# The running sum of a depthwise convolution on VectorE: from SBUF to a two-bank PSUM tile

## The chip, the cores and the metric
The kernel runs on one core of one Trainium2 chip. The metric is the device time of one execution in microseconds (us), the median of several runs; lower is better. The kernel computes in fp32, with every matmul operand split into a high and a low part, so that most products are three matmuls.

## The reference, cut to what matters
A backbone of two layers over 512 latent and 256 context tokens of 1024 channels. Each layer projects its normed input into four head groups (attention, Fourier mixing, a convolution module, pooling), concatenates them, projects back, and runs a SwiGLU feed-forward. The part that the change touches is the convolution module:

```python
def conv_module(a, dw_w, dw_b, ln_g, ln_b, w_pw):
    glu = a[..., :W_CONV] * jax.nn.sigmoid(a[..., W_CONV:])
    y = lax.conv_general_dilated(glu, dw_w[:, None, :], window_strides=(1,),
        padding=[(CONV_WIDTH // 2, CONV_WIDTH // 2)],
        dimension_numbers=('NWC', 'WIO', 'NWC'), feature_group_count=W_CONV) + dw_b
    y = jax.nn.silu(layer_norm(y, ln_g, ln_b))
    return y @ w_pw
```

CONV_WIDTH is 31 and W_CONV is 256: each of 256 channels is summed over 31 shifted copies of its row, each with its own weight (a tap).

## The kernel before
Channels lie on the 128 partitions, so the 256 conv channels are two blocks. `mix_phase` does the token mixers of one layer, `ffn` the feed-forward. Within `mix_phase` the attention (24 tiles of 128 queries and one head in layer 0, 16 in layer 1) is written out step by step, and other work is handed out between its steps: TensorE work by `fill`, conv taps on VectorE by `pull`, conv taps on ScalarE and GpSimd by `side`. A scheduler then sets the final order on each engine, and each engine works through its own list in that order.

**The taps.** `conv_taps` (L551) computes, per block, `cacc = cacc + tap_j * glu[j : j + cwid]`, one VectorE instruction per tap over 783 columns in layer 0 (512 in layer 1, where only the latent tokens are left). Both tensors it reads, the gated input `glu` and the running sum `ca`, and the one it writes lie in SBUF. VectorE does 31 taps of the first block; of the second block the first 10 (layer 0) or 8 (layer 1) are done by `side_taps` (L568), with the products on ScalarE (`prod`) and the sums on GpSimd (L578), and VectorE adds the remaining 21 or 23. `conv_out` then transposes the sums (`lnT`), normalizes them and feeds the output projection (`wo`).

**The scores.** `Tile.soft` (L874) puts the scores of one tile (up to 768 columns) into a PSUM tile `S` of the pool tag `pb`, which has two buffers of two banks each. VectorE takes the row maximum from it (`st`, L886), ScalarE the exponentials (`pr`, L888); then the buffer is free again. `flip` (L892) transposes the result (`PT`) and multiplies by the values (`pv`). The K transposes (`kT`) that precede the attention use the same two buffers.

**Beside it.** GpSimd makes the low parts of weights (L105), the sums of `side_taps` (L578) and the windows of the pooling (L694, L707); TensorE also makes modulation vectors of a later step (`mod`, `mods`), pooled columns (`pp`), Fourier columns (`u`) and the Fourier products (`g`, `fp`, `fq`). The matmuls of every kind are recorded on L161, transposes on L167.

Of the kernel before, what the change touches and what calls it, by code (L numbers as in the profile page):

```python
# [35 lines left out]

# columns of the packed small vectors, per layer
V_G1, V_G2, V_BM, V_DB, V_LG, V_LB, V_PS, V_TAP, V_QG, V_KG, NV = \
    0, 8, 16, 64, 66, 68, 70, 72, 134, 198, 262

# pacing of the work that runs beside the attention, per layer: pieces of the conv columns that go before it, taps of the
# conv on VectorE before it, first step with taps, taps per step on VectorE and on ScalarE with GpSimd, amount of
# other TensorE work per step, the share of it between scores and values, taps of the conv's second block that ScalarE
# and GpSimd take
Pace = namedtuple("Pace", "cols taps0 step0 taps side fill share side_n")
# [4 lines left out]
def kernel(ctx: ExitStack, tc: tile.TileContext, xT, ctxT, vec, cst, dft,  # L50
# [13 lines left out]

    # working tiles by tag: (columns, buffers)
    tags = {f"x{k}": (768, 1) for k in range(KD)}
# [39 lines left out]

    # ------------------------------------------------------------------ constants
    vt = cp.tile([P, DEPTH * NV + 16], F32, name="vt")
# [31 lines left out]

    # silu(c), silu(c_ctx) as stationary operands padded to 32 columns
    scp = cp.tile([P, KD, 32], F32, name="scp")
# [9 lines left out]
    def behind(i, j):  # L152
        """i goes to its queue no earlier than j to its own"""
        tc.add_manual_dep(i.ins, j.ins.name, mybir.DependencyInfo(
            mybir.DependencyClass.NoSync, mybir.DependencyReason.DATA), reason="order")
# [19 lines left out]

    # ------------------------------------------------------------------ weights in order of use
    queue, ready = [], {}
# [104 lines left out]

    # ------------------------------------------------------------------ adaLN modulation
    def scaled_gain(l, i, k0, k1):
# [4 lines left out]
    def mod_pairs(l, q0, q1, mix=True):  # L289
        """pairs q0..q1 of modulation chunks: four groups of two contraction chunks side by side, then their sum"""  # L290
        def fetch_w(q):
            raws = []
            for k in range(0, KD if q < q1 else 0, 4 if mix else 3):
                raw = W("wm", F32) if mix else U("wm", "pr")
                n = min(KD - k, 4 if mix else 3)
                nc.sync.dma_start(out=raw[:, 0:256 * n].rearrange("p (k c) -> p k c", k=n),
                                  in_=rows(w_mod[l, P * k:P * k + P * n, 256 * q:256 * q + 256]))
                raws += [raw[:, 256 * i:256 * i + 256] for i in range(n)]
            return raws

        def finish(q, me):
            ps = PF("mods")
            for c in range(2):
                tr(ps[:, 128 * c:128 * c + 128], me[:, 128 * c:128 * c + 128], ident)
            m2 = modT[l][:, 2 * q:2 * q + 2, :]
            dve.tensor_reduce(out=m2, in_=ps[:, 0:256].rearrange("p (c g w) -> p c w g", c=2, g=4)[:, :, 0:2, :], axis=AX.X, op=ALU.add)
            dve.tensor_tensor(out=m2, in0=m2, in1=vcol(l, V_BM + 2 * q, 2).unsqueeze(2).to_broadcast([P, 2, 2]), op=ALU.add)
            if q // 4 in (1, 4):
                scaled_gain(l, q // 12, 2 * q % 8, 2 * q % 8 + 2)
        raws = fetch_w(q0)  # L310
        yield 0
        prev = None
        for q in range(q0, q1):
            ps = PF("mod")
            for k in range(KD):
                g = k % 4
                mm(ps[32 * g:32 * g + 32, 0:256], scp[:, k, :], raws[k],
                   start=k < 4, stop=k >= 4, tile_position=(0, 32 * g))
            raws = fetch_w(q + 1)
            if prev is not None:  # L320
                finish(*prev)
            me = S("me")
            act.copy(out=me[:, 0:256], in_=ps[:, 0:256])
            prev = q, me
            yield 1.0
        finish(*prev)

    def quarter_load(l, q):
        """columns of the first norm's shift and scale for contraction chunks 2q, 2q+1 of the mixers"""
        out = []  # L330
        for k in range(KD):
            if q % 2 == 0:
                if k % 2 == 0:
                    raw = W("wm", F32)
                v = raw[:, 512 * (k % 2):512 * (k % 2) + 512]
            else:
                v = U("wm", ("g0", "g1", "c0", "c1", "u0", "u1", "b0", "b1")[k])[:, 0:512]
            src = w_mod[l, P * k:P * k + P, 0:2048].rearrange("p (j c) -> p j c", j=2)
            nc.sync.dma_start(out=v.rearrange("p (j c) -> p j c", j=2), in_=src[:, :, 256 * q:256 * q + 256])
            out.append(v)  # L340
        return out
# [21 lines left out]

    # ------------------------------------------------------------------ RMS norms
    class Norm:
        """reciprocal RMS per token on all partitions; squares of chunks below `direct` are added off the tensor engine"""

# [64 lines left out]
    class Acts:  # L432
        """split activations, channels on partitions: latent and context tiles per channel chunk"""

# [14 lines left out]

    # ------------------------------------------------------------------ token mixers  # L450
    def rope_tables(l):
# [11 lines left out]
    def head_norm(t, ng, w):  # L463
        """rows of t hold ng groups of HD: divide each by its rms, in place"""
        sq = U("hsq", "t")
# [10 lines left out]
    def rope(t, na, nh, a0, i):  # L476
        """t: [P, na, nh, HD] of token chunks a0.., tables rtab[2i], rtab[2i+1]; in place"""
        w = na * nh * HD
# [16 lines left out]
    def mix_phase(l, norm, A, filler):  # L495
# [6 lines left out]

        # query, key and value columns: tokens on partitions, contraction outermost
        pl = [PB("qkv") for _ in range(2)]
# [21 lines left out]

        # Q: tile j holds latent chunks 2j, 2j+1 and context chunk 4+j; V split
        ksb = U("ksb", "a0")
# [19 lines left out]
        def tap(b, j):  # L548
            return vcol(l, V_TAP + CONVW * b + j)

        def conv_taps():  # L551
            for b in range(2):
                while done[0] <= b:
                    yield None
                if b:
                    for _ in side:
                        pass
                for j in range((0, pace.side_n)[b], CONVW):
                    if j == 0:
                        yield dve.tensor_scalar(out=cacc[b][:, :cwid], in0=glu[b][:, 0:cwid], scalar1=tap(b, 0),  # L560
                                                scalar2=vcol(l, V_DB + b), op0=ALU.mult, op1=ALU.add)
                    else:
                        yield dve.scalar_tensor_tensor(out=cacc[b][:, :cwid], in0=glu[b][:, j:j + cwid], scalar=tap(b, j),  # L563
                                                       in1=cacc[b][:, :cwid], op0=ALU.mult, op1=ALU.add)

            tdone[0] = True

        def side_taps():  # L568
            """the first taps of the second block: products on ScalarE, sums on GpSimd"""
            while done[0] < 2:  # L570
# [15 lines left out]

        # token-major columns
        def token_major(nm, chunks, sink, PS=PA):
# [18 lines left out]
        for j in range(2):  # L607
# [3 lines left out]
            rope(qsb[j], 2, 4, 2 * j, 0)  # L611
        # K stacks [k_hi;k_hi] and [k_lo;k_lo] over the 128 partitions
        K1 = [U(f"K1{h}", f"x{h}", F32R) for h in range(NKV)]
# [16 lines left out]

        # conv columns: output channels on partitions
        glu = [U(f"glu{b}", f"g{b}") for b in range(2)]
# [44 lines left out]

        # pooled columns: channels on partitions, zero-padded token axis
        ubs = [U(f"ub{b}", f"b{b}") for b in range(2)]
# [170 lines left out]

        # attention over tiles of 128 queries and one head, in three stages run two tiles apart
        qTs = {}
# [14 lines left out]
        class Tile:  # L867
            """128 queries of chunk q and one head"""

# [22 lines left out]
            def flip(self, pt_):  # L892
                """P transposed, the keys of chunks 0..3 in pt_[0] and of 4, 5 in pt_[1], each for two heads"""
                e = self.h % 2
# [127 lines left out]

        # output projection, gated residual, squares for the next norm
        n2 = Norm("b")
# [53 lines left out]

    # ------------------------------------------------------------------ SwiGLU
    def ffn(l, norm, first, second, A, filler):  # L1080
# [5 lines left out]
        def glu(c, pa_, pg, sl):  # L1086
            """h[:, sl] = silu(a) * g, split"""
            hh, hlo = h[c]
# [168 lines left out]
def _pack(i):  # L1257
    """small vectors laid out with channels on the partitions"""
    cols = []
# [38 lines left out]
```

## Time and profile before

| what | value |
|---|---|
| median of 3 runs | 1514.17 us (1511.99 to 1514.2) |
| profiled execution, span from first to last instruction | 1513.7 us (no other time is listed for it) |
| TensorE matmuls (PE) | 1455.2 us busy, 96% |
| weight loads (PEld) | 1210.9 us, 80% |
| VectorE (DVE) | 812.5 us, 54% |
| ScalarE (ACT) | 541.6 us, 36% |
| GpSimd (POOL) | 215.4 us, 14% |

The shares are means over the whole program. Layer 0's mixers run from about 75 to 300 us, its feed-forward to about 905 us, layer 1's mixers to about 1125 us, the rest is its feed-forward. [...] A wait is listed with what ended it.

### The profile page before, as it was taken

To read this page: it belongs to the slowest core of one execution; us is meant where nothing else is said; L and a number is where in the kernel's file an instruction comes from. 1 tells how busy PE (TensorE), PEld (TensorE's weight loads), DVE (VectorE), ACT (ScalarE), POOL (GpSimd) and SP (SyncE) were. 2 spreads that over 40 slices of the span, in tenths; PEclk is the share of its full clock that TensorE was granted. 3 is DMA by queue.
4 is the path that set the end of the run, shared out by engine and by line. 5 is a ranking of instruction groups with operands and counts; after the bars stand their busy time and mean duration, and the time that the engine had idled before them with its cause. 6 is when DMAs were issued, how large, how long until landed. Compare 5 with 4: busy or idle time off the path is not lost.

```text
span 1513.7 us, 20632 instructions
## 1 busy us (share of the span) xinstructions
PE 1455.2 (96%) x8538; PEld 1210.9 (80%) x8538; DVE 812.5 (54%) x1204; ACT 541.6 (36%) x876; POOL 215.4 (14%) x161
## 2 busy tenths in 40 slices
PE   7998899999999999999999999789999999999998
PEld 4786677888888888888888877577789888888887
DVE  3599884346543444344344357699446544444444
ACT  5456566534222112111211234557554322222220
POOL 2435520420000000000000024261140000000000
PEclk9998999999999999999999999999999999999999
DMA  8524344321222123212321222335832423333331
GB/s 297 166 91 138 116 156 124 90 70 57 84 84 84 59 81 111 85 52 88 98 85 56 70 98 56 125 113 162 250 91 73 123 88 94 97 98 97 98 98 56
DMA packets 192926, 157.35 MB, mean 104 GB/s; under 512 B 6464, under 2 KB 179520, under 8 KB 192832
## 3 DMA queue, kind: packets, MB, share of 16 engines
q1 hardware_dynamic: 192544, 155.34, 33.5%
q8 instruction: 67, 1.10, 0.3%
q10 hardware_dynamic: 288, 0.69, 0.1%
q14 instruction: 27, 0.22, 0.0%
HBM read 151.81 MB, written 4.19 MB: 103 GB/s over the span
## 4 chain that ended last, share of the span: by engine, by line
PE 80%; DVE 13%; DMA 3%; ACT 2%; issue 1%; POOL 1%; SPq 0%; DVEq 0%; ACTq 0%
PE ag L161 33%; PE fo L161 20%; PE agc L161 7%; PE wo L161 6%; DVE ca L563 6%; PE mod L161 3%; PE qkv L161 2%; PE ssq L161 2%; PE pv L161 1%; DVE st L886 1%; PE u L161 1%; DMA wi<-in_w_in_dram 1%; PE PT L167 1%; PE S L161 1%; DVE xt L426 1%
## 5 line engine op out<-in xcount | busy, mean ns | idle before, releaser
L1149 DVE SCALAR_TENSOR_TENSOR x<-fo,mod,x 128x512 f32<-128x512 f32 (+1 forms) x264 | 172.2, 661 | 138.4 <-PE fo L161 138.1
L161 PE MATMUL fo<-hh,foh 128*128 128x512 f32 (+1 forms) x528 | 188.2, 357 | 1.9 <-DVE ht L1092 1.9
L161 PE MATMUL fo<-hh,fol 128*128 128x512 f32 (+1 forms) x528 | 187.9, 356 | 0.0
L161 PE MATMUL fo<-hl,foh 128*128 128x512 f32 (+1 forms) x528 | 187.8, 356 | 0.0
L182 ACT CAST foh<-fo 128x1024 fp32r<-128x1024 f32 x44 | 46.2, 1049 | 275.2 <-PE fo L161 218.6
L161 PE MATMUL ag<-xfh,fah 128*128 128x512 f32 (+1 forms) x368 | 140.4, 386 | 1.2 <-ACT xfh L428 1.2
L161 PE MATMUL ag<-xfl,fah 128*128 128x512 f32 (+1 forms) x368 | 140.7, 382 | 0.8 <-DVE xfl L429 0.8
L161 PE MATMUL ag<-xfh,fal 128*128 128x512 f32 (+1 forms) x368 | 140.5, 382 | 0.0
L161 PE MATMUL ag<-xfh,fgh 128*128 128x512 f32 (+1 forms) x368 | 140.0, 381 | 0.0
L161 PE MATMUL ag<-xfh,fgl 128*128 128x512 f32 (+1 forms) x368 | 140.0, 380 | 0.0
L161 PE MATMUL ag<-xfl,fgh 128*128 128x512 f32 (+1 forms) x368 | 139.8, 380 | 0.0
L563 DVE SCALAR_TENSOR_TENSOR ca<-glu,vt,ca 128x783 f32<-128x783 f32 (+1 forms) x104 | 129.8, 1253 | 1.3
L161 PEld LDWEIGHTS fo<-hh,foh 128*128 128x128 f32 x528 | 98.9, 188 | 19.0 <-DVE ht L1092 2.1
L161 PEld LDWEIGHTS fo<-hl,foh 128*128 128x128 f32 x528 | 99.3, 188 | 16.7
L161 PEld LDWEIGHTS fo<-hh,fol 128*128 128x128 f32 x528 | 99.4, 188 | 15.7
L105 DVE TENSOR_TENSOR fal<-fa,fah 128x1024 fp32r<-128x1024 f32 x42 | 51.7, 1232 | 100.9 <-ACT fah L182 100.9
L105 DVE TENSOR_TENSOR fgl<-fg,fgh 128x1024 fp32r<-128x1024 f32 x42 | 51.4, 1225 | 97.6 <-ACT fgh L182 92.7
L182 ACT CAST fah<-fa 128x1024 fp32r<-128x1024 f32 x44 | 46.2, 1049 | 100.4 <-DMA fa<-in_w_ffn_in_dram 86.3
L182 ACT CAST fgh<-fg 128x1024 fp32r<-128x1024 f32 x44 | 46.1, 1048 | 98.5 <-DMA fg<-in_w_ffn_in_dram 88.2
L161 PEld LDWEIGHTS ag<-xfh,fah 128*128 128x128 f32 x368 | 69.0, 188 | 15.0 <-ACT xfh L428 1.4
L161 PEld LDWEIGHTS ag<-xfl,fah 128*128 128x128 f32 x368 | 69.2, 188 | 14.4 <-DVE xfl L429 1.7
L161 PEld LDWEIGHTS ag<-xfh,fgl 128*128 128x128 f32 x368 | 69.2, 188 | 13.1
(333 smaller groups left out, 3159.8 us busy)
## 6 DMA issues: line engine op xcount, KB each, us to landing
wm<-in_w_mod_dram SPq DMA_DIRECT2D x64, 512.0 KB, 4.7
fa<-in_w_ffn_in_dram SPq DMA_DIRECT2D x44, 512.0 KB, 3.9
fg<-in_w_ffn_in_dram SPq DMA_DIRECT2D x44, 512.0 KB, 3.9
fo<-in_w_ffn_out_dram SPq DMA_DIRECT2D x44, 512.0 KB, 3.3
wm<-in_w_mod_dram SPq DMA_DIRECT2D x40, 256.0 KB, 5.7
wo<-in_w_out_dram SPq DMA_DIRECT2D x16, 512.0 KB, 5.0
wm<-in_w_mod_dram SPq DMA_DIRECT2D x16, 384.0 KB, 5.8
x<-in_xT_dram SPq DMA_DIRECT2D x16, 256.0 KB, 4.4
```

The lines of the kernel that those rows point to most:

```text
L105: eng.tensor_tensor(out=out, in0=full, in1=b32(hi), op=ALU.subtract)
L161: i = last_pe[0] = pe.matmul(*a, **kw)
L167: i = last_pe[0] = pe.transpose(*a)
L182: act.copy(out=hi[:, :n], in_=raw[:, :n])
L426: dve.scalar_tensor_tensor(out=t[:, 0:n], in0=x[k][:, sl], scalar=aT[l][:, i, k, s:s + 1], in1=R[:, 0:n], op0=ALU.mult, op1=ALU.mult)
L563: yield dve.scalar_tensor_tensor(out=cacc[b][:, :cwid], in0=glu[b][:, j:j + cwid], scalar=tap(b, j), in1=cacc[b][:, :cwid], op0=ALU.mult, ...
L886: dve.tensor_reduce(out=st[:, 0:1], in_=ps[:, 0:kw], axis=AX.X, op=ALU.max, negate=True)
L1149: dve.scalar_tensor_tensor(out=x[m][:, sl], in0=ps[:, :n], scalar=modT[l][:, 40 + m, st:st + 1], in1=x[m][:, sl], op0=ALU.mult, op1=ALU.add)
```

## The change
The running sum of the taps that VectorE does is no longer kept in `ca` but in a PSUM tile `run`, taken from the tag `pb`, that is, one of the two buffers of the score tiles, for each block from its first VectorE tap to its last. The first tap writes `run` (in the second block it reads the ScalarE and GpSimd sum from `ca`), those between read and write `run`, and the last reads `run` and writes `ca`. So a tap in between reads one tensor from SBUF (`glu`) and one from PSUM. Comments are dropped too, and lines below L556 move by 3 (the taps are L562 and L565 afterwards, the row maximum L889).

```diff
+                run = PB("run")[:, :cwid]
+                j0 = (0, pace.side_n)[b]
+                for j in range(j0, CONVW):
-                for j in range((0, pace.side_n)[b], CONVW):
                     if j == 0:
-                        yield dve.tensor_scalar(out=cacc[b][:, :cwid], in0=glu[b][:, 0:cwid], scalar1=tap(b, 0),
+                        yield dve.tensor_scalar(out=run, in0=glu[b][:, 0:cwid], scalar1=tap(b, 0),
                                                 scalar2=vcol(l, V_DB + b), op0=ALU.mult, op1=ALU.add)
                     else:
-                        yield dve.scalar_tensor_tensor(out=cacc[b][:, :cwid], in0=glu[b][:, j:j + cwid], scalar=tap(b, j),
-                                                       in1=cacc[b][:, :cwid], op0=ALU.mult, op1=ALU.add)
+                        yield dve.scalar_tensor_tensor(out=cacc[b][:, :cwid] if j == CONVW - 1 else run,
+                                                       in0=glu[b][:, j:j + cwid], scalar=tap(b, j),
+                                                       in1=cacc[b][:, :cwid] if j == j0 else run, op0=ALU.mult, op1=ALU.add)
```

No instruction is added or removed among the taps, but the scheduler lays all engines' lists out anew. Three places:

VectorE in layer 0, where the second block's taps begin. Before (`ca_661` is that block's sum, `mod` the modulation, `qst` a split of queries):

```order
L889 RECIPROCAL st<-st 128x1
L901 COPY pt<-PT 128x256
L306 TENSOR_REDUCE mod_99<-mods 128x4
L307 TENSOR_TENSOR mod_99<-mod_99,vt 128x4
L563 SCALAR_TENSOR_TENSOR ca_661<-glu_752,vt,ca_661 128x783
L860 TENSOR_TENSOR qst<-q_640,qst 128x4x64
L563 SCALAR_TENSOR_TENSOR ca_661<-glu_752,vt,ca_661 128x783 x4
L886 TENSOR_REDUCE st<-S 128x1
```

In the changed kernel the same taps begin here (`py`, `pyl` are pooling, `mxl`, `mxcl` low parts of the mixer output):

```order
L711 SCALAR_TENSOR_TENSOR py<-ps,cs,ub_957 64x776 x2
L750 SCALAR_TENSOR_TENSOR mxl_972<-pm,vt,mxh_964 128x512
L892 RECIPROCAL st<-st 128x1
L565 SCALAR_TENSOR_TENSOR run<-glu_752,vt,ca_661 128x783
L750 SCALAR_TENSOR_TENSOR mxcl_988<-pm,vt,mxch_980 128x256
L105 TENSOR_TENSOR pyl<-py,pyh 128x776
L565 SCALAR_TENSOR_TENSOR run<-glu_752,vt,run 128x783
L892 RECIPROCAL st<-st 128x1
L565 SCALAR_TENSOR_TENSOR run<-glu_752,vt,run 128x783
L750 SCALAR_TENSOR_TENSOR mxl_973<-pm,vt,mxh_965 128x512
```

Before, the second block's first tap stood after the 8th of the 24 row maxima; now it stands after the 16th, among the pooling's and the Fourier part's last steps. In layer 1 it moves in the same way, from after the 4th of the 16 to after the 12th.

VectorE at the beginning of layer 1's attention, before (`q`, `rp`, `hs` are the query norms and rotations, `ksl` the low part of K that the K transposes need) and then in the changed kernel:

```order
L560 TENSOR_SCALAR ca_8168<-glu_8257,vt 128x512
L468 TENSOR_REDUCE hs<-hsq 128x8
L488 TENSOR_TENSOR q_8149<-q_8149,rt_103 128x512
L563 SCALAR_TENSOR_TENSOR ca_8168<-glu_8257,vt,ca_8168 128x512
L472 RECIPROCAL hs_8205<-hs_8203 128x8
L489 TENSOR_TENSOR q_8149<-q_8149,rp 128x512
L563 SCALAR_TENSOR_TENSOR ca_8168<-glu_8257,vt,ca_8168 128x512
L474 TENSOR_TENSOR q_8150<-q_8150,hs_8205 128x512
L860 TENSOR_TENSOR qst<-q_8149,qst 128x4x64
L563 SCALAR_TENSOR_TENSOR ca_8168<-glu_8257,vt,ca_8168 128x512
L486 TENSOR_TENSOR rp<-q_8150,rt_104 128x256 x2
L620 TENSOR_TENSOR ksl_8218<-ksb,ksh_8217 128x768
```

```order
L863 TENSOR_TENSOR qst<-q_8151,qst 128x4x64
L486 TENSOR_TENSOR rp<-q_8152,rt_104 128x256 x2
L623 TENSOR_TENSOR ksl_8220<-ksb,ksh_8219 128x768
L488 TENSOR_TENSOR q_8152<-q_8152,rt_103 128x512
L489 TENSOR_TENSOR q_8152<-q_8152,rp 128x512
L623 TENSOR_TENSOR ksl_8224<-ksb,ksh_8223 128x768
L658 TENSOR_TENSOR glu_8260<-cv,glu_8260 128x512
L863 TENSOR_TENSOR qst<-q_8151,qst 128x4x64
L562 TENSOR_SCALAR run<-glu_8259,vt 128x512
L565 SCALAR_TENSOR_TENSOR run<-glu_8259,vt,run 128x512
L889 TENSOR_REDUCE st<-S 128x1
L565 SCALAR_TENSOR_TENSOR run<-glu_8259,vt,run 128x512 x3
```

Seven taps of the first block stood ahead of the second `ksl` before; now both `ksl` come first and no tap begins before the K transposes are through with the two `pb` buffers.

TensorE in layer 0, two scores in a row before, and two neighbouring scores in the changed kernel, with buffer numbers:

```order
L161 MATMUL S_1464<-K11_708,qT_1294 128x512
L161 MATMUL S_1464<-K21_710,qT_1294 128x512
L161 MATMUL S_1464<-K11_708,qT_1294 128x256
L161 MATMUL S_1464<-K21_710,qT_1294 128x256
L161 MATMUL S_1584<-K11_708,qT_1294 128x512
L161 MATMUL S_1584<-K21_710,qT_1294 128x512
```

```order
L161 MATMUL S_1123<-K21_710,qT_1007 128x256
L167 MATMUL PT_1223<-ident_81,pr_1068 128x128 x4
L167 MATMUL PT_1229<-ident_81,pr_1068 128x128 x2
L161 MATMUL mod_1134<-wm_1081,scp_96 32x256 x4
L161 MATMUL mod_1134<-wm_1083,scp_96 32x256 x4
L161 MATMUL pv_1233<-pt_1167,vsb_641 64x128 x8
L161 MATMUL pv_1233<-pt_1168,vsb_641 64x128
L161 MATMUL S_1179<-K11_708,qT_1007 128x512
```

While `run` holds one buffer, the next score's matmuls wait until the one before has been read by ScalarE, and no two scores stand next to each other in that time; this gap is the narrowest of the eight of layer 0's first block.

## Rows read from the trace of the kernel before

**Rows 1.** The page's chain that ended last, by line.
```profile
PE ag L161 33%; PE fo L161 20%; PE agc L161 7%; PE wo L161 6%; DVE ca L563 6%; PE mod L161 3%; PE qkv L161 2%; PE ssq L161 2%; PE pv L161 1%; DVE st L886 1%; PE u L161 1%; DMA wi<-in_w_in_dram 1%; PE PT L167 1%; PE S L161 1%; DVE xt L426 1%
```

**Rows 2.** Stretches in layer 0: length, busy us of each engine, granted clock, DMA.
```profile
120.00:140.00 20.00, 17.14 (x139) 13.20 (x132) 19.86 (x19) 12.35 (x21) 14.46 (x7) 0.91 0.38 119
140.00:160.00 20.00, 15.47 (x110) 11.66 (x112) 17.73 (x24) 12.41 (x22) 11.93 (x10) 0.83 0.20 65
160.00:180.00 20.00, 14.38 (x138) 12.46 (x130) 16.30 (x11) 7.52 (x14) 16.78 (x12) 0.98 0.51 159
180.00:212.00 32.00, 31.74 (x280) 25.26 (x281) 27.65 (x47) 17.35 (x37) 7.37 (x6) 0.91 0.46 148
212.00:257.00 45.00, 41.08 (x343) 31.98 (x341) 26.64 (x66) 31.85 (x77) 2.37 (x1) 0.92 0.36 109
```

**Rows 3.** Line L563: its instructions (ns min/median/max), and its busy time in a stretch.
```profile
L563 DVE SCALAR_TENSOR_TENSOR ca<-glu,vt,ca x104: 725/1025/3157, 95.6 to 1041.9; 128x512 f32<-128x512 f32 x53, 128x783 f32<-128x783 f32 x51
...
120.00:180.00 60.00, 37.56 (x20) 0.91 0.36 114
```

**Rows 4.** Timeline (start us, us): a tap on DVE, and POOL beside it.
```profile
135.19 2.53 DVE L563 SCALAR_TENSOR_TENSOR ca<-glu,vt,ca 128x783 f32<-128x783 f32 x1
134.29 2.60 POOL L578 TENSOR_TENSOR ca<-ca,prod 128x783 f32<-128x783 f32 x1
```

**Rows 5.** Timeline: two DVE instructions inside one on POOL.
```profile
219.28 0.47 DVE L747 SCALAR_TENSOR_TENSOR mxcl<-pm,vt,mxch 128x256 fp32r<-128x256 f32 x1
219.69 2.32 DVE L105 TENSOR_TENSOR pyl<-py,pyh 128x776 fp32r<-128x776 f32 x1
218.82 2.37 POOL L105 TENSOR_TENSOR wol<-wo,woh 128x1024 fp32r<-128x1024 f32 x1 [6.83 <-ACT woh L182]
```

**Rows 6.** Groups on DVE by form: count, busy us, mean ns, idle before.
```profile
L563 DVE SCALAR_TENSOR_TENSOR ca<-glu,vt,ca 128x783 f32<-128x783 f32 x51 | 74.6, 1462 | 0.8
L747 DVE SCALAR_TENSOR_TENSOR mxl<-pm,vt,mxh 128x512 fp32r<-128x512 f32 x2 | 1.5, 751 | 1.5 <-ACT mxh L746 1.5
L563 DVE SCALAR_TENSOR_TENSOR ca<-glu,vt,ca 128x512 f32<-128x512 f32 x53 | 55.3, 1053 | 0.5
```

**Rows 7.** Stretches in layer 1, columns as in group 2.
```profile
960.00:980.00 20.00, 14.27 (x64) 11.18 (x62) 15.16 (x25) 9.64 (x14) 5.04 (x2) 0.91 0.44 141
980.00:1000.00 20.00, 17.34 (x97) 13.25 (x98) 19.68 (x24) 14.09 (x22) 13.04 (x9) 0.83 0.26 79
1000.00:1020.00 20.00, 15.86 (x125) 12.78 (x124) 19.93 (x27) 9.65 (x19) 12.93 (x11) 0.91 0.33 103
1064.00:1091.00 27.00, 27.00 (x289) 18.87 (x288) 14.38 (x44) 17.48 (x35) 2.36 (x1) 1.00 0.84 258
```

**Rows 8.** Waits of PE, total us, times, longest; layer 0, then layer 1.
```profile
PE S L161 <- ACT pr L888: 5.5, 1, 5.5
PE PT L167 <- DVE pt L901: 4.5, 1, 4.5
...
PE kT L167 <- DVE ksl L620: 3.7, 1, 3.7
PE pv L161 <- DVE pt L901: 3.1, 1, 3.1
```

**Rows 9.** Who uses the score tile S: ns min/median/max of each.
```profile
L886 DVE TENSOR_REDUCE st<-S x40: 415/946/959, 109.0 to 1072.5; 128x1 f32<-128x768 f32 x32, 128x1 f32<-128x256 f32 x8
L888 ACT ACTIVATE pr<-S,st x40: 466/902/941, 109.9 to 1077.8; 128x768 f32<-128x768 f32 x32, 128x256 f32<-128x256 f32 x8
L888 ACT ACTIVATION_READ_ACCUMULATOR pr<-S,st x40: 188/193/238, 110.7 to 1078.6; 128x1 f32 x40
```

**Rows 10.** Matmuls on PE between two scores: pieces of the chain (start us, us).
```profile
192.56 0.81 PE PT L167 x6
196.67 1.00 PE mod L161 x16
230.20 1.52 PE pv L161 x24
```

## The prediction

> **What bounds the kernel now.** I read the chain that ended last first: matmuls hold most of it, but the taps on VectorE (`ca`) hold 6% [rows 1], some 90 us of 1513.7, and they can only lie in the two attention stretches. So the second view is the busy time by stretches there. Between 120 and 180 us TensorE stands still for 2.9, 4.5 and 5.6 us of each 20 while VectorE is busy for 19.9, 17.7 and 16.3 [rows 2]; in layer 1 from 960 to 1020 it stands still for 5.7, 2.7 and 4.1 us [rows 7]. In the feed-forward, two thirds of the span, the change touches nothing. The third view is the tap itself: the median of 104 is 1.03 us, the shortest (512 columns) 0.725, the longest 3.16 [rows 3]. The mean of the 783-column form is 1.46, of the 512-column form 1.05 [rows 6]. The fourth view, the timeline, shows where the long ones lie: a tap of 2.53 us stands beside a GpSimd instruction that began before it [rows 4]. The same is seen without taps: inside one GpSimd instruction from 218.8 to 221.2, a VectorE instruction with one operand in PSUM and one in SBUF took 0.47 us, and right behind it one with both in SBUF took 2.32 [rows 5]. So what is slow is a VectorE instruction with two SBUF tensors beside GpSimd, and the taps are such. Last, the waits show what TensorE waits for: scores behind the exponentials 5.5, a transpose behind a VectorE copy 4.5, in layer 1 the K transposes behind `ksl` 3.7 and `pv` behind a copy 3.1 [rows 8]; all of them hang on VectorE instructions queued behind taps.
>
> **The tap's price.** In the changed kernel a tap reads `glu` from SBUF and `run` from PSUM, as the 0.47 us instruction does. Its undisturbed price: reading one operand from PSUM costs 751 ns against the shortest tap's 725 at 512 columns [rows 3, 6], so +0.03 us. That gives 1.05 us for 783 columns (median 1.025 of all taps, most of the shorter half being 512 wide, is my value for the undisturbed one) and 0.76 for 512. Writing to PSUM from VectorE stands in no row. I take nothing for it; as the upper end I take four times the reading surcharge, 0.10 per tap, and no gain below, since the PSUM row is the longer one. VectorE then saves 74.6 - 51 x 1.05 = 21 us in layer 0 and 55.3 - 53 x 0.76 = 15 us in layer 1. The two first taps and the two that still read the block's earlier sum from `ca` are priced alike.
>
> [...] The row's surcharge is 26 ns. [...]
>
> **The sum.**
> - A, layer 0, 120 to 180 us: 20 taps took 37.6 us there [rows 3] and would take 21. TensorE stands still for 13.0 us, and the clock, granted at 0.91, 0.83 and 0.98 [rows 2], withholds (0.09 + 0.17 + 0.02) x 20 = 5.6 us more. I take 10 of the idle time and 4 of the clock: -14. Ends: -5 and -18.6.
> - B, 180 to 212 us: hardly idle, but the clock at 0.91 withholds 2.9 [rows 2]; fewer stalls ahead of it, and its second-block taps moved away: -2 (0 to -2.9).
> - E, layer 1, 960 to 1020 us: 12.5 us idle, 7.0 withheld [rows 7]. The 3.7 for `ksl` goes because seven taps leave the place ahead of it, the 3.1 of `pv` because the queue is shorter; the first idle microseconds precede the taps and stay. -7 and -3 of the clock: -10 (-4 to -15).
> - C, the second block in layer 0 comes late. Its 21 taps, 22 us, now lie between the 16th row maximum and the norm, about 212 to 257 us, where VectorE is busy for 26.6 of 45 [rows 2], 18.4 free. That is 3.7 too much even if nothing waits, and the Fourier products and scores there wait for VectorE results with a tap in front: +6 (3.7 to 20).
> - F, the same in layer 1: 23 taps, 17.5 us, into 1064 to 1091, where VectorE has 27 - 14.4 = 12.6 free [rows 7] and TensorE has been busy throughout. 4.9 too much; as 11 of the taps follow the last row maximum and only the norm waits for them, I take +3 (0 to 12).
> - D, one score buffer instead of two. From a score's end its buffer is free after 0.95 (row maximum) + 0.90 + 0.19 (exponentials) = 2.0 us, or 3.1 with a whole tap in front [rows 9]. In the narrowest gap of layer 0's first block TensorE has 0.81 + 1.00 + 9/12 of 1.52, together 2.95 us, to do [rows 10]; the other gaps mostly hold 12 or more wide matmuls. So the wait that takes the place of the old ones is mostly covered: +2 (0 to 8). If TensorE ran out of such work, each of the 26 scores under one buffer would cost up to 3 us.
>
> DMA queues, GpSimd and ScalarE get the same instructions; GpSimd's own, stretched too, get shorter, but nobody waits for it now. Sum: -14 - 2 - 10 + 6 + 3 + 2 = -15. The profiled span of 1513.7 gives 1498.7; the median of the runs is 0.5 higher, 1514.17, so I say **1499**. A difference under about 0.2%, 3 us, can't be told from none.
>
> **The rivals.**
> - *Everything comes back*: idle time and clock of A, B and E in full, but 3 us of layer 1's beginning, and of the late costs only C's 3.7. 13.0 + 5.6 + 2.9 + 12.5 + 7.0 - 3 - 3.7 = 34: 1480. For it: TensorE has work in all these stretches. Against: VectorE stays three quarters busy.
> - *Slower: the late block*. In C and F TensorE waits for short VectorE results, by the list of the changed kernel 26 in layer 0 (8 row maxima, 8 copies of transposes, 4 and 6 Fourier steps) and 20 in layer 1. If each is held up by one tap, that is 26 x 1.05 + 20 x 0.76 = 42 us. The gains with D are -24, so it turns slower once over 24 of these 42, 57%, reach TensorE. At three quarters, 31 us: 1521. For it: VectorE is over-full in both stretches by the sum. Against: most of these results have other matmuls beside them.
> - *The contention stays*, because a tap still reads one SBUF tensor and a scalar beside GpSimd: then the change doesn't do to a tap what I say. The moved taps still leave GpSimd's stretch (2.4 us busy from 212 to 257 [rows 2]), so half of A and E less the late costs: -12 + 11, about 1513. Against it stands the 0.47 us row [rows 5].
> - *PSUM is dear*: 0.10 more per tap, 10 us on VectorE, half of it on the path: 1504.
>
> **The numbers.** Forecast 0.58, with a range of its own from 1488 to 1510. Everything comes back 0.12, the late block 0.13, contention stays 0.08, PSUM dear 0.09. Faster: 0.58 + 0.12 + 0.06 of the dear case = 0.76. Same: 0.05 of contention, 0.03 of dear, 0.01 of the late block: 0.09. The rest, 0.15, is slower. The range that leaves out 2 in 10, on both sides, is 1483 to 1516.
>
> **What would show it.** Right: taps of about 1.05 and 0.76 us with a maximum near the median, also beside GpSimd; idle time of TensorE between 120 and 180 down to a few microseconds; no wait of the K transposes for `ksl` in layer 1; VectorE nearly full in the 45 us before layer 0's norm, with TensorE waiting there some 5 us more than now. Wrong: taps of 2 to 3 us left, undisturbed taps over 1.15 us, or scores waiting for ScalarE for more than 8 us in all.

## The result, and the profile after the change

| kernel | median of runs | span of the profiled execution | PE busy, us | DVE busy, us | POOL busy, us |
|---|---|---|---|---|---|
| before | 1514.18 us, 4 runs (1511.99 to 1515.82) | 1513.7 us | 1455.2 | 812.5 | 215.4 |
| changed | 1497.48 us, 4 runs (1496.42 to 1500.52) | 1494.6 us | 1450.2 | 778.7 | 198.3 |

The ratio is 0.9888 with a 95% interval of 0.9873 to 0.9904: faster by 1.1%, some 17 us. The forecast was 1499. The profiled execution took 1496.42 us, about 1 us less than the median, so its rows show a little more gain than the runs.

First the taps, by line: count, shortest, median and longest in ns, answering to [rows 3], and then by form (count, busy us, mean ns), answering to [rows 6].

```profile
L565 DVE SCALAR_TENSOR_TENSOR run<-glu,vt,run x98: 729/756/1042, 106.0 to 1067.5; 128x512 f32<-128x512 f32 x50, 128x783 f32<-128x783 f32 x48
L565 DVE SCALAR_TENSOR_TENSOR ca<-glu,vt,run x4: 731/880/1028, 158.0 to 1068.7; 128x783 f32<-128x783 f32 x2, 128x512 f32<-128x512 f32 x2
L565 DVE SCALAR_TENSOR_TENSOR run<-glu,vt,ca x2: 752/1748/2743, 206.8 to 1041.4; 128x783 f32<-128x783 f32 x1, 128x512 f32<-128x512 f32 x1
```

```profile
L565 DVE SCALAR_TENSOR_TENSOR run<-glu,vt,run 128x783 f32<-128x783 f32 x48 | 49.4, 1030 | 0.4
L565 DVE SCALAR_TENSOR_TENSOR run<-glu,vt,run 128x512 f32<-128x512 f32 x50 | 37.4, 749 | 0.6
L307 DVE TENSOR_TENSOR mod<-mod,vt 128x4 f32<-128x4 f32 x40 | 14.5, 368 | 0.5
```

The 98 taps whose sum lies in PSUM have no long ones left: 1042 ns at most, where it was 3157 before [rows 3]. 19 of the 98 begin inside a GpSimd instruction that has 0.3 us or more still to run, and take their usual time all the same. The one long tap is a second block's first, which still reads the earlier sum from SBUF: 2743 ns. All 104 together take 49.4 + 37.4 us, 3.5 for the four last taps and 3.5 for the two that read `ca`: 93.8 instead of 129.9 [rows 6]. The third row of the second view is the bias of the modulation, both operands in SBUF. It has become longer; before it stood as

```profile
L307 DVE TENSOR_TENSOR mod<-mod,vt 128x4 f32<-128x4 f32 x40 | 10.5, 264 | 0.6
```

The timeline of the changed kernel shows why (start us, us):

```profile
128.78 2.53 POOL L105 TENSOR_TENSOR wil<-wi,wih 128x1024 fp32r<-128x1024 f32 x1 [1.07 <-ACT wih L182]
128.97 2.35 DVE L307 TENSOR_TENSOR mod<-mod,vt 128x4 f32<-128x4 f32 x1
131.25 1.03 DVE L565 SCALAR_TENSOR_TENSOR run<-glu,vt,run 128x783 f32<-128x783 f32 x1
131.26 1.88 POOL L581 TENSOR_TENSOR ca<-ca,prod 128x783 f32<-128x783 f32 x1
```

Four values a partition, both operands in SBUF, take 2.35 us and end with the GpSimd instruction beside them. The tap that follows, beside the next GpSimd instruction, takes its 1.03 us. It is the picture of [rows 4], with another victim.

TensorE over the same stretches of layer 0 as [rows 2], then layer 1, moved 12 us earlier than [rows 7] because all work there stands that much earlier:

```profile
120.00:140.00 20.00, 19.48 (x183) 15.36 (x182) 18.39 (x26) 17.30 (x29) 12.74 (x7) 1.00 0.52 160
140.00:160.00 20.00, 15.49 (x125) 11.83 (x124) 19.16 (x27) 13.61 (x24) 14.31 (x13) 1.00 0.40 132
160.00:180.00 20.00, 20.00 (x189) 16.82 (x188) 6.18 (x14) 10.49 (x21) 8.56 (x9) 1.00 0.51 159
180.00:212.00 32.00, 28.71 (x242) 22.94 (x243) 20.11 (x39) 19.58 (x38) 7.76 (x7) 0.95 0.54 169
212.00:257.00 45.00, 42.20 (x334) 32.45 (x333) 37.44 (x85) 28.62 (x75) 2.38 (x1) 0.96 0.38 111
...
948.00:968.00 20.00, 14.96 (x76) 11.87 (x75) 13.43 (x23) 13.78 (x20) 6.65 (x4) 0.96 0.40 130
968.00:988.00 20.00, 20.00 (x124) 13.98 (x125) 17.51 (x28) 13.24 (x23) 12.71 (x13) 0.95 0.33 102
988.00:1008.00 20.00, 18.94 (x187) 16.16 (x183) 17.28 (x31) 11.37 (x23) 6.70 (x7) 1.00 0.54 173
```

From 120 to 180 us TensorE stands still for 0.5 + 4.5 + 0 = 5.0 us instead of 13.0, at full granted clock; in layer 1 for 5.0 + 0 + 1.1 = 6.1 instead of 12.5. VectorE now is busy for 37.4 of the 45 us from 212 to 257, where it was 26.6. What TensorE waits for, longest first, in layer 0 (90 to 255 us) and in layer 1 (930 to 1110 us), answering to [rows 8]:

```profile
PE pv L161 <- DVE pt L904: 2.6, 2, 2.1
PE mods L167 <- ACT me L323: 2.6, 2, 2.4
PE pm L161 <- DVE mxcl L750: 2.3, 1, 2.3
PE S L161 <- ACT qT L868: 0.7, 1, 0.7
PE S L161 <- ACT pr L891: 0.5, 1, 0.5
```

```profile
PE S L161 <- ACT K L632: 2.6, 1, 2.6
PE pm L161 <- DVE pyl L105: 2.4, 1, 2.4
PE cv L161 <- ACT glu L657: 2.3, 1, 2.3
PE pw L161 <- ACT csh L957: 1.9, 1, 1.9
...
PE kT L167 <- DVE ksl L623: 0.6, 1, 0.6
```

The scores' wait for the exponentials has gone from 5.5 to 0.5 us, although one score buffer is missing while taps run; in layer 1 the K transposes wait 0.6 instead of 3.7 us for `ksl`, and the wait of `pv` for a copy is gone. Other waits of 2 us and more stand there now.

### The profile page after: what moved, and what is told of

It is laid out like the page before. It is cut to its first block, busy times and chain, and to the rows that moved or that the text cites. A ratio compares the mean times of both kernels' runs of the same rounds, so it can differ in the third digit from the quotient of the medians.

```text
span 1494.6 us, 20629 instructions
## 1 busy us (share of the span) xinstructions
PE 1450.2 (97%) x8538; PEld 1207.1 (81%) x8538; DVE 778.7 (52%) x1204; ACT 541.4 (36%) x876; POOL 198.3 (13%) x161
## 4 chain that ended last, share of the span: by engine, by line
PE 85%; DVE 7%; ACT 3%; DMA 2%; POOL 1%; issue 1%; SPq 0%; DVEq 0%; ACTq 0%
PE ag L161 33%; PE fo L161 21%; PE agc L161 7%; PE wo L161 6%; PE mod L161 3%; PE qkv L161 2%; DVE run L565 2%; PE u L161 2%; PE ssq L161 2%; PE cv L161 1%; PE S L161 1%; PE pv L161 1%; DMA wi<-in_w_in_dram 1%; PE PT L167 1%; PE pp L161 1%
## 5 line engine op out<-in xcount | busy, mean ns | idle before, releaser
L565 DVE SCALAR_TENSOR_TENSOR run<-glu,vt,run 128x512 f32<-128x512 f32 (+1 forms) x98 | 86.9, 887 | 1.1
L161 PEld LDWEIGHTS ag<-xfl,fah 128*128 128x128 f32 x368 | 69.2, 188 | 14.2 <-DVE xfl L429 1.4
```

The costliest lines, as they stand in the source:

```text
L161: i = last_pe[0] = pe.matmul(*a, **kw)
L565: yield dve.scalar_tensor_tensor(out=cacc[b][:, :cwid] if j == CONVW - 1 else run, in0=glu[b][:, j:j + cwid], scalar=tap(b, j), in1=cacc[b ...
```

## The experiments

Ratios are to the kernel before, run beside it on the same chip; a ratio times 1514 gives the us. Every diff is against the changed kernel unless it says otherwise. The theory: the gain is that a tap with one SBUF input isn't stretched beside GpSimd. The rivals: the new order makes the gain, or the late second block and the missing score buffer take a good part of it back.

### The order without the operand (e1_hold_only)
```diff
-   out=cacc[b][:, :cwid] if j == CONVW - 1 else run
+   out=run if j == j0 else cacc[b][:, :cwid]
-   in1=cacc[b][:, :cwid] if j == j0 else run
+   in1=run if j == j0 + 1 else cacc[b][:, :cwid]
+                dve.memset(run[:, 0:1], 0.0)
```


> The first tap still writes the PSUM tile and the tile is held until after the last tap, but all taps in between keep their sum in SBUF: the lists of all engines nearly those of the changed kernel, the taps' operands those of the kernel before. Theory 1 (the gain is the shorter tap beside GpSimd): taps of 2 to 3 us come back, their sum is near 130 us as before, and with the late second block the time is 1514 or more, up to 1530. Theory 2 (the gain is the new order: K transposes ahead of the taps, the second block out of GpSimd's stretch): the time stays within 4 us of the changed kernel, 1494 to 1502. In between, 1503 to 1511, each would hold a part.

The `memset` behind the last tap does no work for the result; it keeps the PSUM tile held until there. Measured: 1518.43 us, ratio 1.0027 (1.0014 to 1.0039). Both `ksl` stand ahead of layer 1's taps and the second blocks begin after the 16th and the 12th row maximum, as in the changed kernel. Its taps by form:

```profile
L565 DVE SCALAR_TENSOR_TENSOR ca<-glu,vt,ca 128x783 f32<-128x783 f32 x48 | 64.7, 1348 | 0.3
L565 DVE SCALAR_TENSOR_TENSOR ca<-glu,vt,ca 128x512 f32<-128x512 f32 x50 | 48.5, 971 | 0.5
```

Long taps are back, though less than before (119 us for all instead of 129.9, since the late block meets less of GpSimd), and the new order with them is slower than the kernel before. So the order brings nothing by itself; theory 2 falls.

### One layer alone (e2_layer0)
```diff
-                run = PB("run")[:, :cwid]
+                run = cacc[b][:, :cwid] if last else PB("run")[:, :cwid]
```


> Only layer 0's taps use PSUM. By the terms of the prediction layer 0 gives A + B + C and most of D, -14 - 2 + 6 + 1.2 = -9: 1505, and layer 1 the rest. By the positions of the output projections in the two traces layer 0 gives 12 and layer 1 some 6: 1502. If the layers are not independent (a later start of layer 1's weights, say) the time lies outside 1500 to 1507.

Measured: 1504.66 us, ratio 0.9931 (0.9913 to 0.995). Layer 0 gives (1 - 0.9931) x 1514 = 10.4 us, layer 1 the rest to 0.9888, 6.5. The intervals are 3 us wide on either side, so both expectations hold, and the time lies inside 1500 to 1507. Layer 1 was not changed alone: its 6.5 us is a difference, and that the layers add up is not shown.

### Second block early or late, in SBUF or PSUM (e3_first_block, e4_one_run, e7_late_sbuf)
Three runs and the changed kernel make a square. e3:
```diff
-                run = PB("run")[:, :cwid]
+                run = cacc[b][:, :cwid] if b else PB("run")[:, :cwid]
```


> Only the first block of each layer keeps its sum in PSUM; the second keeps it in SBUF and, being free of the score buffers, begins after the 8th row maximum again. Theory 1a (the late second block costs some 9 us, as predicted with C and F): the time is 1489 plus what the second block's stretched taps cost beside GpSimd, at most 12 of them by 1 us, so 1489 to 1498. Theory 1b (the late block costs under 3 us): the stretched taps come on top of the changed kernel's time, 1498 to 1507.

e4:
```diff
-                run = PB("run")[:, :cwid]
+                run = PB("run")[:, :cwid] if not b else run
```


> One PSUM tile for both blocks of a layer, held from the first tap of the first to the last of the second: every tap stays in PSUM, and the second block begins after the 8th row maximum again. Theory 1a (the late second block costs some 9 us): 1488 to 1491, the idle time of TensorE in 200 to 220 us gone. Theory 1b (it costs under 3 us): 1495 to 1498. Theory 3 (one score buffer is the dear part): slower than the changed kernel, since the buffer is missing for as many or more tiles without a pause: 1499 or more.

e7:
```diff
-   out=cacc[b][:, :cwid] if j == CONVW - 1 else run
+   out=(run if j == j0 else cacc[b][:, :cwid]) if b else cacc[b][:, :cwid] if j == CONVW - 1 else run
-   in1=cacc[b][:, :cwid] if j == j0 else run
+   in1=(run if j == j0 + 1 else cacc[b][:, :cwid]) if b else run
+                if b:
+                    dve.memset(run[:, 0:1], 0.0)
```


> The first block's sum stays in PSUM as in the change; the second block takes its PSUM tile as late as in the change and holds it, but keeps its sum in SBUF from the second tap on. With the runs so far this fills the square of early or late, SBUF or PSUM for the second block (early, SBUF: 1509.6; early, PSUM: 1497.0; late, PSUM: 1497.5). Theory 1 (only the meeting with GpSimd counts): the late block meets little of GpSimd's work, its taps have means under 1.2 and 0.85 us, and the time is 1497 to 1502. Rival (PSUM operands are worth the same wherever the taps stand): 1506 or more.

Measured:

| second block | sum in SBUF | sum in PSUM |
|---|---|---|
| early, after the 8th row maximum of layer 0 | e3: 1509.61, 0.9973 (0.9961 to 0.9986) | e4: 1497.02, 0.9885 (0.9861 to 0.9908) |
| late, after the 16th | e7: 1497.31, 0.9887 (0.9872 to 0.9902) | changed: 1497.48, 0.9888 (0.9873 to 0.9904) |

The second block's taps at 783 columns in e3 and in e7:

```profile
L565 DVE SCALAR_TENSOR_TENSOR ca<-glu,vt,ca 128x783 f32<-128x783 f32 x21 | 28.5, 1358 | 0.2
```

```profile
L565 DVE SCALAR_TENSOR_TENSOR ca<-glu,vt,ca 128x783 f32<-128x783 f32 x19 | 19.6, 1031 | 0.0
```

The same instruction takes 1.36 us in GpSimd's stretch and 1.03 behind it (at 512 columns, in layer 1, 0.88 and 0.85 us, so the late place isn't quite free of GpSimd there). For the second block PSUM or a place away from GpSimd do equally well; only early and in SBUF is dear. Late against early, both in PSUM, makes 0.0003 x 1514 = 0.5 us, and the intervals leave room for some 4 us either way: the 9 us that I had put on lateness are not there (theory 1a falls). The 0.5 us is a net figure, for in e4 VectorE is busy for 18.8 of the 20 us from 160 to 180, where it is 6.2 in the changed kernel. In e4 one score buffer is missing for both blocks without a pause, and it isn't slower, so theory 3 falls as well. e3 was slower than either expectation: its stretched taps add 28.5 - 21 x 1.03 = 6.9 us in layer 0 and, by the same sum, 3 us in layer 1, and it is 0.0088 x 1514 = 13 us behind e4, give or take 4. So the 10 us on VectorE reach the time about in full; that a stretched microsecond costs more than one is not shown.

e1 and e7 differ only in the first block's sum: 1.0027 against 0.9887, 21 us. The first block, which can't get away from GpSimd, is what needs PSUM.

### Input or output (e5_alternate)
```diff
-   out=cacc[b][:, :cwid] if j == CONVW - 1 else run
+   out=cacc[b][:, :cwid] if (CONVW - 1 - j) % 2 == 0 else run
-   in1=cacc[b][:, :cwid] if j == j0 else run
+   in1=cacc[b][:, :cwid] if j == j0 or (CONVW - j) % 2 == 0 else run
```


> The sum goes to and fro: a tap reads the sum from SBUF and writes it to PSUM, the next reads it from PSUM and writes it to SBUF. Theory 1 (two SBUF inputs make a tap slow beside GpSimd, the output doesn't matter): the taps that read SBUF have a mean of 1.3 us and more at 783 columns (0.9 and more at 512) with a maximum over 2 us, the others 1.03 and 0.75 with a maximum within 10% of that. Rival (any two SBUF operands, the output among them): both kinds have maxima over 2 us. The time lies between the two kernels, 1500 to 1512, or by the rival 1510 to 1518.

Measured: 1510.9 us, ratio 0.9981 (0.997 to 0.9993), which lies in both ranges and decides nothing; the taps do. The two kinds of tap:

```profile
L565 DVE SCALAR_TENSOR_TENSOR run<-glu,vt,ca x51: 730/1032/3090, 102.1 to 1083.1; 128x512 f32<-128x512 f32 x26, 128x783 f32<-128x783 f32 x25
L565 DVE SCALAR_TENSOR_TENSOR ca<-glu,vt,run x51: 718/749/1054, 103.9 to 1085.2; 128x512 f32<-128x512 f32 x26, 128x783 f32<-128x783 f32 x25
```

They lie in turn in the same stretches. Those that read two SBUF tensors reach 3.09 us, with means of 1.28 us (1.3 was expected) and 0.95; those that read one and write to SBUF never pass 1.054, though 12 of them begin inside a GpSimd instruction: the inputs decide, not the output.

### GpSimd's sums made small (e6_small_sums)
Against the kernel before:
```diff
-   pool.tensor_tensor(out=cacc[1][:, :cwid], in0=cacc[1][:, :cwid], in1=m[:, :cwid], op=ALU.add)
+   pool.tensor_tensor(out=cacc[1][:, :4], in0=cacc[1][:, :4], in1=m[:, :4], op=ALU.add)
```


> The kernel before, but GpSimd's sums of the side taps are taken over 4 columns instead of 783 or 512, so that the output leaves those products out; GpSimd's sums were 29.6 us, 18.0 of it in layer 0's attention. The operands of VectorE's taps are those of the kernel before. Theory 1 (GpSimd's own work stretches the taps): the taps' sum falls from 130 us to 100 to 115 us and the time to 1500 to 1509. Rival (the taps are slow for a reason of their own, SBUF operands as such): the sum stays over 122 us and the time within 4 us of the kernel before.

Measured: 1506.4 us, ratio 0.9951 (0.9936 to 0.9966). The taps with both inputs in SBUF:

```profile
L563 DVE SCALAR_TENSOR_TENSOR ca<-glu,vt,ca 128x783 f32<-128x783 f32 x51 | 64.9, 1272 | 0.8
L563 DVE SCALAR_TENSOR_TENSOR ca<-glu,vt,ca 128x512 f32<-128x512 f32 x53 | 49.5, 942 | 0.6
```

64.9 + 49.5 = 114.4 us instead of 129.9, without touching a tap's operands, and 7 us off the time, both as theory 1 has it. What GpSimd does is the cause; beside the rest of its work (low parts of weights, pooling) taps still take up to 3.06 us here.

### Another victim freed (e8_mod_psum)
Against e4:
```diff
+            m1 = ps[:, 256:260].rearrange("p (c w) -> p c w", c=2)
-            dve.tensor_reduce(out=m2, in_=ps[:, 0:256]...
+            dve.tensor_reduce(out=m1, in_=ps[:, 0:256]...
-            dve.tensor_tensor(out=m2, in0=m2, in1=vcol(l, V_BM + 2 * q, 2)...
+            dve.tensor_tensor(out=m2, in0=m1, in1=vcol(l, V_BM + 2 * q, 2)...
```


> One PSUM tile for both blocks of a layer as in the run before, and the modulation's reduce (4 values a partition) leaves its result in PSUM, so that the addition of the bias behind it (40 times, mean 329 ns, up to over 2 us, 13.2 us in all) has one SBUF input. Theory 1 (any VectorE instruction with two SBUF inputs is held by GpSimd): its mean falls under 150 ns, VectorE loses some 8 us of busy time, and the time falls by 0 to 4 us, to 1493 to 1497. Rival (the hold passes to the next such instruction): VectorE's sum falls by under 4 us and the time stays at 1496 to 1499.

Measured: 1498.66 us, ratio 0.9892 (0.9876 to 0.9909), not to be told from e4. The bias by line (ns), and a pooling step by form, in e4 and in e8:

```profile
L308 DVE TENSOR_TENSOR mod<-mods,vt x40: 142/161/163, 129.3 to 1071.4; 128x4 f32<-128x4 f32 x40
```

```profile
L105 DVE TENSOR_TENSOR pyl<-py,pyh 128x512 fp32r<-128x512 f32 x2 | 2.0, 1021 | 0.0
L105 DVE TENSOR_TENSOR pyl<-py,pyh 128x512 fp32r<-128x512 f32 x2 | 3.5, 1762 | 0.0
```

40 instructions of up to over 2 us became 40 of at most 163 ns, as theory 1 has it (mean 157, where it said under 150). They take 6.3 us instead of 13.2, but VectorE's sum fell by only 778.5 - 775.2 = 3.3 us: `pyl`, with two SBUF inputs, grew by 1.5 us at 512 columns, and the pooling steps `py` by 1.6. The hold went on to other instructions, as the rival has it on VectorE's sum. The time shows no gain, but with some 4 us of room either way it can't tell 0 from theory 1's smaller gains.

### More or fewer taps on ScalarE and GpSimd (e9 to e12)
Side taps per layer; e9 keeps the changed kernel's tiles, the others have e4's one tile:
```diff
-PACE = (Pace(12, 6, 3, 2, 4, 3.0, 0.7, 10), Pace(8, 10, 2, 2, 2, 3.0, 0.3, 8))
+PACE = (Pace(12, 6, 3, 2, 4, 3.0, 0.7, 14), Pace(8, 10, 2, 2, 2, 3.0, 0.3, 12))   (e9; e10: 5 and 4; e11: 0 and 0; e12: 3 and 2)
```


> The change, with 14 and 12 instead of 10 and 8 of the second block's taps on ScalarE and GpSimd: four fewer taps on VectorE in the late block of each layer, 4.2 and 3.0 us, and eight more products and sums. Theory 1 (VectorE, 19.4 and 19.6 of 20 us busy from 200 to 240, still holds TensorE there): faster than the change by 2 to 5 us, 1493 to 1496. Rival (what holds TensorE there is the pooling's chain, not the taps, and GpSimd's added sums stretch what else reads SBUF): 1497 to 1501.

> One PSUM tile for both blocks of a layer, with 5 and 4 instead of 10 and 8 of the second block's taps on ScalarE and GpSimd: nine fewer sums on GpSimd, some 15 us of its work beside which other VectorE instructions are stretched, nine fewer products on ScalarE, and nine more taps on VectorE, 5.2 and 3.0 us. Theory 1 (what GpSimd and ScalarE lose is worth more than the added taps): 1492 to 1496. Rival (VectorE, 18 to 19.7 of 20 us busy from 120 to 180 with one tile for both blocks, is the bound there): 1498 to 1503.

> One PSUM tile for both blocks of a layer, and all 31 taps of both blocks on VectorE: GpSimd's sums and ScalarE's products are gone, 18 of each, and VectorE has 10 and 8 more taps than in the change, 10.3 and 6.0 us. Theory 1 (GpSimd's help costs more beside VectorE than it saves): the time is that of 5 and 4 side taps or less, 1488 to 1493. Rival (VectorE, 18 to 19.7 of 20 us busy from 120 to 200 with 5 side taps, is then the bound): the taps run on past 210 us and the time is 1495 or more.

> As the run with none, but with 3 and 2 side taps. By theory 1 between 1488 and 1493 and not above the run with 5 and 4; by the rival 1494 to 1497, between that run and the one with none.

Measured:

| side taps, layers 0 and 1 | median us | ratio |
|---|---|---|
| e9: 14, 12 | 1503.83 | 0.993 (0.9912 to 0.9948) |
| changed: 10, 8 | 1497.48 | 0.9888 (0.9873 to 0.9904) |
| e4: 10, 8 | 1497.02 | 0.9885 (0.9861 to 0.9908) |
| e10: 5, 4 | 1492.93 | 0.9857 (0.9841 to 0.9872) |
| e12: 3, 2 | 1496.17 | 0.9883 (0.9863 to 0.9902) |
| e11: 0, 0 | 1495.59 | 0.9877 (0.9858 to 0.9896) |

More side taps cost 6 us, outside both expectations. Part of it stands behind layer 0's norm, where `csl`, with two SBUF inputs, meets GpSimd's low parts twice in e9 (266.73 and 270.55 us):

```profile
266.73 2.54 DVE L105 TENSOR_TENSOR csl<-cs,csh 128x768 fp32r<-128x768 f32 x1 [3.20 <-ACT csh L957]
270.55 2.54 DVE L105 TENSOR_TENSOR csl<-cs,csh 128x768 fp32r<-128x768 f32 x1 [1.27 <-ACT csh L957]
```

In the changed kernel the first of the two took 0.96 us, and there `pw` waits for neither; in e9 it waits for them for 2.4 us. Idle time is the smaller part of the loss, though: of the 7.9 us by which e9's profiled span is longer, 1457.0 - 1450.2 = 6.8 are longer matmul time, at a mean granted clock of 0.990 against 0.993. What lowered the clock was not traced. e10 has the lowest ratio of all kernels. Its stretch from 140 to 160 us, where the changed kernel still loses 4.5 us, stands below that of e4, from which it differs in the side taps alone:

```profile
140.00:160.00 20.00, 16.16 (x126) 12.76 (x124) 19.69 (x25) 14.19 (x25) 13.59 (x11) 0.94 0.29 95
140.00:160.00 20.00, 19.41 (x159) 15.30 (x161) 19.70 (x29) 11.99 (x23) 6.63 (x6) 1.00 0.45 141
```

TensorE stands still for 0.6 instead of 3.8 us, with GpSimd busy for 6.6 instead of 13.6 us and ScalarE for 12.0 instead of 14.2. VectorE is just as full, so it wasn't VectorE's load that TensorE waited for there; whether GpSimd's or ScalarE's share did it is open. e10's interval lies just under the changed kernel's but overlaps those of e4, e11 and e12: that fewer side taps do no harm is shown, that 5 and 4 are the best is not. In e11 the last tap of layer 0 starts at 210.7 us instead of 188.0 in e4, so VectorE is late there, as the rival has it, and its time falls just inside the rival's, like e12's.

## Why the prediction was right, step by step

**The tap's price** held: 1.03 and 0.75 us, against 1.05 and 0.76. VectorE's saving on taps is 74.6 - (49.4 + 2.7 + 2.0) = 20.5 and 55.3 - (37.4 + 1.5 + 0.8) = 15.6 us, against 21 and 15. Writing to PSUM, which no row had shown, cost nothing at 783 columns: 1030 ns against 1031 for the same tap in SBUF away from GpSimd (e7). The surcharge of 26 ns for reading doesn't show either, neither there nor at 512 columns, where the median is 747 ns against 752 for the 53 taps of the kernel before, some of them held. I had priced the two first taps of the second blocks like the others; one took 2.7 us.

**A and E** held in size in their own stretches. A: 13.0 + 5.6 withheld by the clock before, 5.0 and nothing now, -13.6 against -14. E: 12.5 + 7.0 before, 6.1 and (0.04 + 0.05) x 20 = 1.8 now, -11.6 against -10. Both reasons named for E show in layer 1's waits: `ksl` costs 0.6 us now, and `pv` isn't found. But the waits for `pyl` (2.4) and `csh` (1.9) stand just behind E's stretch. The sums over 180 us of layer 1, from 940 us before and from 928 us now, take them in:

```profile
sum 180.00, PE 162.13 PEld 127.91 DVE 123.55 ACT 102.23 POOL 58.79; mean PE 20.27 PEld 15.99 DVE 15.44 ACT 12.78 POOL 7.35
sum 180.00, PE 166.26 PEld 131.93 DVE 114.47 ACT 106.72 POOL 59.58; mean PE 20.78 PEld 16.49 DVE 14.31 ACT 13.34 POOL 7.45
```

Over these 180 us the idle time fell from 17.9 to 13.7, by 4.1 us and not by E's 6.4. By layer, e2 gives 10.4 and 6.5 us, where the forecast's terms give 9 and 6.

**B** did not come. From 180 to 212 us TensorE stands still for 3.3 instead of 0.3 us, and the clock withholds 0.05 x 32 = 1.6 instead of 2.9: +1.7 instead of -2. Most of it belongs to the late block, as the next step shows.

**C and F**, the late blocks, were wrong in mechanism. VectorE did become as full as forecast, 37.4 of 45 us, but that is no loss of TensorE's: it stands still for 2.8 us there, against 3.9 before [rows 2], and run e4, which moves the blocks back, gains 0.5 us, not 9. What the late block does cost in layer 0 is a single event just ahead of that stretch, by the timeline of the changed kernel:

```profile
206.33 2.36 POOL L105 TENSOR_TENSOR wol<-wo,woh 128x1024 fp32r<-128x1024 f32 x1 [6.83 <-ACT woh L182]
206.79 2.74 DVE L565 SCALAR_TENSOR_TENSOR run<-glu,vt,ca 128x783 f32<-128x783 f32 x1
209.44 0.47 DVE L750 SCALAR_TENSOR_TENSOR mxcl<-pm,vt,mxch 128x256 fp32r<-128x256 f32 x1
209.97 0.58 PE L161 MATMUL pm<-pyh,smh 128*128 128x256 f32 x1 [2.25 <-DVE mxcl L750]
```

The block's first tap, the one that still has two SBUF inputs, meets GpSimd, `mxcl` queues behind it, and TensorE waits 2.25 us. e4 has no tap in that place and waits 1.7 us for `pyl` instead. In layer 1 the late taps begin at 1041 us, and `pw` waits 1.9 us for `csh` of the norm behind them; e4, whose taps end earlier, has the same 1.9 us, so that isn't the price of lateness. The step that failed is the one that took VectorE's excess, 3.7 and 4.9 us, as lost "even if nothing waits": an excess in a stretch costs only where somebody waits at its end.

**D** was covered as said: 0.5 us of waiting for the exponentials, against +2.

**The clock** was the other mis-sized part, and it hid C and F. Of the span, 1513.7 - 1494.6 = 19.1 us went: 1455.2 - 1450.2 = 5.0 us of it as shorter matmul time, 14.1 as idle time. The forecast had 9 us of clock (4 + 2 + 3) and 17 of idle time with 11 given back, 6 net. So 4 us too much on the clock and 8 too little on idle time left an error of 4 in the profiled execution, and 1.5 between the medians: that the time came out so near is in part luck, two errors of opposite sign. The idle time of A and E alone fell by 8.0 + 6.4 = 14.4 us, so the rest of the program stands still no longer than before in sum. On the clock, A and E withheld 5.6 + 5.2 us less, but a clock below 1.00 was granted in other places instead. (The granted clock is a share of full speed: the single microseconds from 128 to 168 us of the kernel before read 1.00 or 0.50, all but four.) So it was behind the late taps of layer 1, here before and in the changed kernel:

```profile
1091.00:1120.00 29.00, 28.67 (x148) 23.28 (x147) 11.06 (x21) 13.99 (x20) 12.18 (x6) 1.00 0.43 119
1079.00:1108.00 29.00, 26.44 (x151) 22.13 (x150) 11.19 (x21) 14.98 (x22) 12.35 (x8) 0.94 0.32 91
```

Over the whole profiled execution the mean granted clock is 0.988 before and 0.993 now, some 18 and 10 us withheld. These 8 us gave back at most 5.0: what the granted clock withholds over a stretch counts its idle time too, and is an upper end of what it costs, not its price. The prediction took 9 of 15.5 us, a share that no row had given. Whether idle time explains all of the difference is open.

**The rivals.** "Everything comes back" has the right idea of the late block, but 4.5 us of idle time stay at 140 to 160, beside waits for a modulation copy on ScalarE (`me`, 2.4) and for `pt` (2.1); with fewer side taps, in e10, that idle time is down to 0.6. "The contention stays" is refuted by e5. "Slower: the late block" fell with e4. "PSUM is dear" fell with the tap's price.

## What to carry to other kernels

If VectorE works beside GpSimd, count the SBUF inputs of each VectorE instruction: here taps with two reached 3.09 us and taps with one 1.054 (e5), and a sum in PSUM, or a place where GpSimd is mostly idle, took the hold away at no price per tap (means of 1030 and 1031 ns at 783 columns, in the changed kernel and in e7). The hold then fell in part on other instructions with two SBUF inputs (in e8 `pyl` at 512 columns went from 1021 to 1762 ns), so freeing one pays only if TensorE waits for it (that is argued; e8 freed one for which it doesn't), and ask whether GpSimd's help is still worth having: after the change, 10 and 8 side taps were no faster than none (e4 and e11); what they were worth before it was not measured. Don't price a fuller engine as lost time; find who waits for its last instruction.

## What the runs showed of the hardware

A VectorE instruction over 4 values a partition took 2.35 us beside GpSimd, longer than a tap of 783: it ended at 131.32 us, the GpSimd instruction beside it at 131.31, so this hold lasted as long as GpSimd's instruction still ran. One-input instructions can be held too: the norm's step `zt` over 256 columns, in place in SBUF, in the changed kernel (ns, shortest, median, longest):

```profile
L942 DVE TENSOR_SCALAR zt<-zt,mv x10: 402/408/2520, 257.6 to 1085.0; 128x256 f32<-128x256 f32 x10
```

One of layer 0's six, which begin at 257.6 us and meet GpSimd's low parts, took 2520 ns instead of 408. And the first tap, the same kind of instruction, at 512 columns took longer into PSUM than into SBUF, before and now:

```profile
L560 DVE TENSOR_SCALAR ca<-glu,vt 128x512 f32<-128x512 f32 x1 | 0.5, 539 | 0.0
```

```profile
L562 DVE TENSOR_SCALAR run<-glu,vt 128x512 f32<-128x512 f32 x1 | 0.8, 801 | 0.0
```

At 783 columns it took 1101 and 1097 ns, no difference. Why the 262 ns show at 512 columns and not at 783 was not shown, nor why this `zt` was held where taps with one SBUF input were not. A first tap of 512 columns comes once in the program, so this costs it a quarter of a microsecond.
